# The first NSA scores ahead of the last query columns, and FoX output, compression and convolution in one block on TensorE

## The chip, the cores and the metric

The kernel runs on one core of a Trainium2 chip. The metric is the device time of one launch in microseconds (us), lower is better. A core has TensorE (PE, matrix products into PSUM), VectorE (DVE), ScalarE (ACT), GpSimd (POOL) and SyncE (SP, which here issues nearly all DMAs). Each engine works through its own list of instructions and waits on the others by semaphores.

## The reference

Two layers over 256 tokens of width 1024. Per layer:

```python
h = rms_norm(x, norm_g)
z = h @ w_in                                   # all inputs of three groups of heads
o_a = fox_attention(fq, fk, fv, ff + fox_b)    # 4 heads of 64, forget-gate bias, causal
o_b = conformer_conv(glu_in, ...)              # GLU, causal depthwise convolution of 31 taps
                                               # on 256 channels, LayerNorm, swish, 256x256 product
o_c = nsa_attention(...)                       # 8 query heads in 2 KV groups; three branches
                                               # mixed by sigmoid gates: compressed blocks,
                                               # selected blocks, sliding window
mixed = concatenate([o_a * silu(f_gate), o_b * silu(c_gate), o_c * silu(n_gate)])
x = x + mixed @ w_out
```

In the compressed branch, blocks of 32 keys (or values) at a stride of 16 go through a two-layer network with GELU, `gelu(blk @ w1) @ w2`; the 15 results are keys and values of their own. At 256 tokens the selected blocks and the window both cover all causal keys. A last RMSNorm follows. All is float32 at the interface.

## The kernel before

Large products are made in three terms of fp32r operands: weights and activations are split into a high and a low part (ACT casts the high part, L238; DVE subtracts for the low part, L242). The input projection is 24 column blocks of 128, each made by `s(i)` (L446 to L459): 24 matmuls of 128x256 into half a PSUM bank, two blocks to a bank. `s(16)` to `s(23)` are the blocks of the SiLU gates.

Weights come by one SP queue in a fixed list (`S_ORDER`, L169). They land in a ring of 6 raw buffers of 512 KB (`RAW`, L19). `pump()` (L214) issues the next load as soon as a raw buffer is free, which is when DVE has made the low part, or, for the weights `w1` of the compression, which are used unsplit, when `compress` has read them. The list has the eight `w1` pieces (four for the keys, four for the values) between blocks S11 and S16. So six of them are in the ring when the compression starts; the last two (`ww_1_2`, `ww_1_3`) and S16, S17, and so on, can only be issued while it runs.

Three steps are made of fp32 matmuls that fill only part of the columns of TensorE's array, several side by side:

- `fox_pv()` (L723): probabilities times values of FoX, 64 columns wide, 8 matmuls.
- `compress(i)` (L784): `w1` for keys (i=0) and values (i=1), 32 wide, 16 matmuls each, 4 to a `w1` piece. ACT then copies the result to `part` (L795).
- `conv()` (L539): the convolution, 32 wide, 64 matmuls.

The records count each fp32 matmul twice (x32, x16 and x128). `hidden()` (L803) multiplies `part` by a small matrix (the two halves of `part`, keys and values, have separate matmuls) and starts GELU on DVE and ACT, `gelu()` ends it, `compressed_kv()` (L823) applies `w2` (tile `pkv`), and `compressed()` (L835) makes the tiles `kcx` and `vbd` of the compressed keys and values, which `cmp_scores(0)` (tile `cs`, in pass n == 2) reads.

`scores(n)` makes the logits of query heads j = n mod 4 of both groups (tile `sw`), `exps(n)` the maximum on DVE and the exponentials on ACT, `norms(n)` the scaling on DVE, `trans(n)` the transposes on TensorE (tile `pt`), `pv(n)` the product with the values (tile `on`). Heads 0 and 1 need `query(0)`, which follows blocks S8 and S9; heads 2 and 3 need `query(1)`, after S10 and S11.

The order on PE, SP and POOL is that of the code. DVE and ACT are ordered by a scheduler that works from modelled times; `mark()` and `behind()` keep the splits from being put too early.

Of the kernel before, what the change touches and what calls it, by code (L numbers as in the profile page):

```python
# [124 lines left out]
def trunk(ctx, tc, a, out, dbg=None):  # L125
# [126 lines left out]
    def need(key, ahead=AHEAD):  # L252

        while key not in split:
            assert split_next(), key
        n = sum(1 for k in split)
        while n < ahead + 1 and split_next():
            n += 1
        return split[key]
# [139 lines left out]
    for l in range(L):  # L399
# [46 lines left out]
        def s(i, ahead=AHEAD):  # L446

            mark()
            hi, lo = need(("S", i, l), ahead)
            if i % 2 == 0:  # L450
                bank[i // 2] = pz(nm(f"ps{i}"))
            o = bank[i // 2][:, (i % 2) * 256:(i % 2 + 1) * 256]
            hi = hi.rearrange("p (k c) -> p k c", k=8)
            lo = lo.rearrange("p (k c) -> p k c", k=8)
            for k in range(8):
                te.matmul(o, hi[:, k], hTh[:, k], start=k == 0, stop=False)  # L456
                te.matmul(o, hi[:, k], hTl[:, k], start=False, stop=False)  # L457
                te.matmul(o, lo[:, k], hTh[:, k], start=False, stop=k == 7)  # L458
            del split["S", i, l]  # L459
# [263 lines left out]
        def fox_pv():  # L723
            ofv = fx["o"] = po(nm("ofx")).rearrange("p (i t) -> p i t", i=2)
            for i in range(2):
                for c, kt in ((slice(0, 256), 0), (slice(256, 384), 1)):
                    for g in range(2):
                        vc = slice((2 * i + g) * 64, (2 * i + g) * 64 + 64)
                        te.matmul(ofv[g * 64:(g + 1) * 64, i, kt * 128:], fv[:, kt, vc], fpts[i, g][:, c],
                                  start=i == 0 and kt == 0, stop=i == 1 and kt == 1)  # L730
# [20 lines left out]
        def query(i):  # L751

            if not qs2:
                qs2.extend(cp.tile([128, 4, 256], F32R, name=nm(f"qs{g}"), tag=f"qs{g}", bufs=1) for g in range(2))
            q = rope(s2(8 + 2 * i), C("ck").unsqueeze(1).broadcast_to([128, 2, 256]),
                     C("sk").unsqueeze(1).broadcast_to([128, 2, 256]), (2, 256), f"q{i}")
            for g, (r, r2) in enumerate(halves):
                hi = qs2[g][r, 2 * i:2 * i + 2]
                sc.mul(hi, q[r], 0.125)
                ve.scalar_tensor_tensor(qs2[g][r2, 2 * i:2 * i + 2], q[r], 0.125, hi.bitcast(F32), op0=ALU.mult,  # L760
                                        op1=ALU.subtract)
# [22 lines left out]
        def compress(i):  # L784

            ph = pscore(nm(f"ph{i}"))
            for q in range(4):
                w = raws.pop(("w1", i, q, l)).rearrange("p (k c) -> p k c", k=4)
                for j in range(4):
                    te.matmul(ph[j * 32:(j + 1) * 32, :256], cm["x", i][:, q * 4 + j, :], w[:, j, :],  # L790
                              start=q == 0, stop=q == 3)
                used(1)
            if i == 0:
                cm["part"] = cp.tile([128, 2, 256], F32, name=nm("part"), tag="tg", bufs=1)
            sc.copy(cm["part"][:, i], ph[:, :256])  # L795
# [7 lines left out]
        def hidden():  # L803
            hT = ppt(nm("hidT"))
            for i in range(2):
                for m in range(2):
                    te.matmul(hT[:, i * 64 + m * 32:i * 64 + m * 32 + 32], cm["part"][:, i, m * 128:(m + 1) * 128],
                              C("s4"), start=True, stop=True)
            ve.tensor_copy(hid, hT[:, :128])
            ve.tensor_tensor(g1, hid, hid, op=ALU.mult)  # L810
            ve.tensor_scalar(g1, g1, 0.044715, 1.0, op0=ALU.mult, op1=ALU.add)
            ve.tensor_tensor(g1, g1, hid, op=ALU.mult)
            sc.activation(g2, g1, AF.Tanh, scale=GELU_C)

        def gelu():
            ve.scalar_tensor_tensor(gk.rearrange("p m c -> p (m c)"), g2[:, 0:64], 1.0, hid[:, 0:64],
                                    op0=ALU.add, op1=ALU.mult)
            hv = hid[:, 64:128].rearrange("p (m n) -> p m n", n=16)
            tv = g2[:, 64:128].rearrange("p (m n) -> p m n", n=16)
            ve.scalar_tensor_tensor(tv, tv, 1.0, hv, op0=ALU.add, op1=ALU.mult)  # L820
            ve.tensor_copy(gv, tv.unsqueeze(2).broadcast_to([128, 4, 4, 16]))
# [51 lines left out]
        def exps(n, gs=(0, 1)):  # L873
            t = n // 4
            nk = 128 * (t + 1)
            if gs[0] == 0:
                Ps[n] = cp.tile([128, 2, 2, nk], F32, name=nm(f"P{n}"), tag="P", bufs=3)
                mxs[n] = cp.tile([128, 4], F32, name=nm(f"mx{n}"), tag="mx", bufs=4)
                sus[n] = cp.tile([128, 4], F32, name=nm(f"su{n}"), tag="su", bufs=4)
            P, mx, su = Ps[n], mxs[n], sus[n]  # L880
            msk = C("mk")[:, 0:128] if t == 0 else C("mk")[:, 128:384]
            for g in gs:
                for b in range(2):
                    c = 2 * g + b
                    masked(P[:, g, b], sb[n][g][b], msk, mx[:, c:c + 1])
                    sc.activation(P[:, g, b], P[:, g, b], AF.Exp, bias=mx[:, c:c + 1], scale=-1.0,  # L886
                                  accum_out=su[:, c:c + 1])
# [174 lines left out]
        keys_split()  # L1062
        s(1)
        blocks()
        s(10, 1)
        compress(0)
        fox_pv()
        compress(1)
        s(11, 1)
        query(1)  # L1070
        hidden()
        gelu()
        load_g(a["norm_g"][1] if l == 0 else a["final_g"], nm("gn"))
        scores(0)
        scores(1)
        exps(0)
        norms(0)
        exps(1)
        need(("S", 17, l), 0)
        conv()  # L1080
        cs = {}
        for n in range(8):
            t = n // 4
            trans(n)
            if n < 7:
                norms(n + 1)
            if n < 2:
                scores(n + 2)
            elif n < 6:
                scores(n + 2, (0,))  # L1090
            if n == 0:
                s(16)
                ln_stats()
                compressed_kv()
                compressed()
                exps(2)
                s(17)
                gates(0)
                mixed(0, 2, fx["o"], 0.5)
            elif n == 1:  # L1100
                s(18)
                exps(3)
                s(19)
                ln_swish()
                gates(1)
            elif n == 2:
                s(20)
                cs[0] = cmp_scores(0)
                exps(4, (0,))
                scores(4, (1,))  # L1110
                s(21)
                pcv = pointwise()
                gates(2)
                mixed(2, 2, pcv, 0.25)
                exps(4, (1,))
            elif n == 3:
                s(22)
                cmp_norm(0, *cs[0])
                exps(5, (0,))
                scores(5, (1,))  # L1120
                s(23)
                cmp_trans(0, cs[0][0])
                mix_split(0, 2)
                mix_split(2, 2)
                gates(3)
                exps(5, (1,))
                cs[1] = cmp_scores(1)
            else:
                if n % 2 == 0:
                    pj = pz(nm(f"pw0{n}"))  # L1130
                if n < 6:
                    need(("O", 2 * n - 3, l), 0)
                    exps(n + 2, (0,))
                ks = range(4) if n % 2 == 0 else range(4, 8)
                project(0, n // 2 - 2, pj, ks[:2])
                if n < 6:
                    scores(n + 2, (1,))
                    exps(n + 2, (1,))
                project(0, n // 2 - 2, pj, ks[2:])
            if n == 4:  # L1140
                cmp_norm(1, *cs[1])
            elif n == 6:
                cmp_trans(1, cs[1][0])
            if n % 2:
                pv(n - 1)
                pv(n)
            if n == 3:
                pv_cmp(0)
                mixed(4, 4, on[0], 0.5, slice(0, 128))
                mix_split(4, 4, slice(0, 128))  # L1150
            if n in (5, 7):
                residual(0, (n - 5) // 2 * 512, 512, pj)
# [96 lines left out]
```

## Time and profile before

| | |
|---|---|
| median of 3 runs | 317.46 us (317.41 to 318.85) |
| the profiled execution | 317.38 us, its span 315.6 us |
| mean granted TensorE clock | 0.997 |
| busy: PE, DVE, ACT, POOL | 304.8, 235.4, 187.1, 22.5 us |
| HBM read | 52.85 MB, 173 GB/s over the span |

The span runs from the first to the last instruction; 1.78 us lie around it. A matmul's busy time is that of one instruction with its fill, and successive matmuls overlap; what a step costs on TensorE is read from the start of its first matmul to the start of the next step's first. The two layers have the same order; times below are of the first.

### The profile page before, as it was taken

Reading aid. Unit: us, or ns where it says so; the run is one execution under the profiler, and the core shown is the slowest. Engines: PE = TensorE matmul, PEld = TensorE weight load, DVE = VectorE, ACT = ScalarE, POOL = GpSimd, SP = SyncE. Lnnn points to the kernel's source line nnn. Section 1 sums busy time; section 2 is a strip of 40 time slices with the busy share of each in tenths; the row PEclk is TensorE's granted clock in tenths of the full one; section 3 lists DMA queues with packets and bytes.
Section 4 is the critical chain, followed back from the end, with each engine's and each line's share of the span. In section 5 each row is a group of like instructions: output and inputs, shape, how many; then the busy total and the mean of one; then the engine's idle time right before and its main releaser. Section 6 shows DMA issues by size and latency. Waiting matters only on the chain.

```text
span 315.6 us, 6707 instructions
## 1 busy us (share of the span) xinstructions
PE 304.8 (97%) x2590; PEld 273.3 (87%) x2590; DVE 235.4 (75%) x627; ACT 187.1 (59%) x408; POOL 22.5 (7%) x50
## 2 busy tenths in 40 slices
PE   8899999999999999999999999999999999999991
PEld 3799999995879999888899999999577999988891
DVE  3847789982799998974573778998199999896532
ACT  4647669650495958761554766874159595786110
POOL 2000034000002000000000003400000200000000
PEclk9999999999999999999999999999999999999998
DMA  7697798905937444230452778880791744000101
GB/s 289 220 382 262 262 256 212 353 3 214 413 111 265 136 135 132 68 93 2 153 180 102 255 251 272 211 316 2 260 409 71 264 133 135 0 2 0 56 15 68
DMA packets 16547, 54.93 MB, mean 174 GB/s; under 512 B 2049, under 2 KB 2433, under 8 KB 16514
## 3 DMA queue, kind: packets, MB, share of 16 engines
q1 hardware_dynamic: 15408, 51.51, 46.6%
q0 software_dynamic: 960, 2.92, 4.1%
q8 instruction: 20, 0.33, 0.4%
q14 instruction: 13, 0.11, 0.1%
q10 hardware_dynamic: 146, 0.07, 0.1%
HBM read 52.85 MB, written 1.64 MB: 173 GB/s over the span
## 4 chain that ended last, share of the span: by engine, by line
PE 89%; issue 4%; DMA 3%; ACT 1%; DVE 1%; POOLq 0%; POOL 0%; DVEq 0%
PE ps L456 15%; PE ps L458 14%; PE ps L457 14%; PE pcn L545 4%; PE pA L429 4%; PE pt L914 4%; PE pB L429 4%; PE pw L977 4%; PE pw L978 4%; PE pw L981 4%; PE on L927 3%; DMA ww<-in_w 3%; PE sw L858 2%; PE sw L859 2%; PE fpt L718 1%
## 5 line engine op out<-in xcount | busy, mean ns | idle before, releaser
L456 PE MATMUL ps<-hTh,wS_1h 128*128 128x256 f32 x192 | 54.4, 283 | 0.0
L456 PE MATMUL ps<-hTh,wS_0h 128*128 128x256 f32 x192 | 54.3, 283 | 0.0
L458 PE MATMUL ps<-hTh,wS_0l 128*128 128x256 f32 x192 | 54.0, 281 | 0.0
L458 PE MATMUL ps<-hTh,wS_1l 128*128 128x256 f32 x192 | 54.0, 281 | 0.0
L457 PE MATMUL ps<-hTl,wS_1h 128*128 128x256 f32 x192 | 54.0, 281 | 0.0
L457 PE MATMUL ps<-hTl,wS_0h 128*128 128x256 f32 x192 | 54.0, 281 | 0.0
L886 ACT ACTIVATE P<-P,mx 128x128 f32<-128x128 f32 (+1 forms) x64 | 28.5, 448 | 15.1 <-DVE mx L481 15.0
L456 PEld LDWEIGHTS ps<-hTh,wS_1h 128*128 128x128 f32 x192 | 36.2, 189 | 0.6 <-issue 0.4
L456 PEld LDWEIGHTS ps<-hTh,wS_0h 128*128 128x128 f32 x192 | 36.2, 189 | 0.6 <-issue 0.4
L457 PEld LDWEIGHTS ps<-hTl,wS_0h 128*128 128x128 f32 x192 | 36.2, 189 | 0.2
L457 PEld LDWEIGHTS ps<-hTl,wS_1h 128*128 128x128 f32 x192 | 36.2, 189 | 0.2
L458 PEld LDWEIGHTS ps<-hTh,wS_1l 128*128 128x128 f32 x192 | 36.2, 189 | 0.0
L458 PEld LDWEIGHTS ps<-hTh,wS_0l 128*128 128x128 f32 x192 | 36.2, 189 | 0.0
L242 DVE TENSOR_TENSOR wS_0l<-wS,wS_0h 128x1024 fp32r<-128x1024 f32 x24 | 28.5, 1220 | 8.3 <-ACT wS_0h L238 8.3
L242 DVE TENSOR_TENSOR wS_1l<-wS,wS_1h 128x1024 fp32r<-128x1024 f32 x24 | 28.5, 1221 | 8.0 <-ACT wS_1h L238 8.0
L238 ACT CAST wS_1h<-wS 128x1024 fp32r<-128x1024 f32 x24 | 24.1, 1052 | 1.8 <-DMA wS<-in_wS 1.8
L238 ACT CAST wS_0h<-wS 128x1024 fp32r<-128x1024 f32 x24 | 24.1, 1051 | 0.5 <-DMA wS<-in_wS 0.4
L481 DVE CUSTOM_DVE_ANT_0 P<-sw,cf 128x128 f32<-128x128 f32 (+1 forms) x64 | 19.4, 354 | 2.4 <-PE sw L859 2.4
L916 ACT COPY PT<-pt 128x512 f32<-128x512 f32 x24 | 13.6, 585 | 9.6 <-PE pt L914 9.6
L984 DVE TENSOR_TENSOR x<-pw,x 128x512 f32<-128x512 f32 (+1 forms) x9 | 5.7, 630 | 16.7 <-PE pw L981 16.7
L484 DVE TENSOR_SCALAR P<-P,co 128x128 f32<-128x128 f32 (+1 forms) x64 | 16.4, 316 | 0.1
L545 PE MATMUL pcn<-yr,cw 128*32 128x256 f32 x256 | 14.2, 380 | 0.0
(241 smaller groups left out, 680.5 us busy)
## 6 DMA issues: line engine op xcount, KB each, us to landing
wS<-in_wS SPq DMA_DIRECT2D x48, 512.0 KB, 5.7
ww<-in_w SPq DMA_DIRECT2D x16, 512.0 KB, 4.8
wO<-in_wo SPq DMA_DIRECT2D x16, 512.0 KB, 3.6
yr<-ybuf POOLq DMA_DIRECT2D x16, 142.0 KB, 5.7
wA<-in_wA SPq DMA_DIRECT2D x4, 420.0 KB, 5.2
wB<-in_wB SPq DMA_DIRECT2D x4, 390.0 KB, 3.9
x<-in_x SPq DMA_DIRECT2D x2, 512.0 KB, 4.1
w<-in_w SPq DMA_DIRECT2D x2, 384.0 KB, 4.4
```

The lines of the kernel that those rows point to most:

```text
L238: behind(E.Activation, lambda: sc.copy(hi, w))
L242: behind(E.DVE, lambda: ve.tensor_tensor(lo, w, hi.bitcast(F32), op=ALU.subtract))
L429: te.matmul(p[:, :n], a_[:, k, tok], b_, start=first, stop=s_ == "t" and k == 7)
L456: te.matmul(o, hi[:, k], hTh[:, k], start=k == 0, stop=False)
L457: te.matmul(o, hi[:, k], hTl[:, k], start=False, stop=False)
L458: te.matmul(o, lo[:, k], hTh[:, k], start=False, stop=k == 7)
L481: ve.tensor_tensor_reduce(o, x, m, -1.0, 3.0e38, ALU.add, ALU.min, mx)
L484: ve.tensor_scalar(x, x, r, None, op0=ALU.mult)
L545: te.matmul(p[g * 32:(g + 1) * 32, i * 256:(i + 1) * 256], w[:, g, q], yr[:, g, 4 * q:4 * q + 256], start=q == 0, stop=q == 7)
L886: sc.activation(P[:, g, b], P[:, g, b], AF.Exp, bias=mx[:, c:c + 1], scale=-1.0, accum_out=su[:, c:c + 1])
L914: te.transpose(pt[:, o + b * 128:o + (b + 1) * 128], Pg[:, b * 128:(b + 1) * 128], C("id"))
L916: sc.copy(PT, pt)
```

## The change

Only the order of calls in the layer's loop changes. The first two score steps with their exponentials move from behind `gelu()` to ahead of `s(10)`; `fox_pv`, both `compress` and `conv` follow `s(11)` in a row, with `conv` between the two `compress`; `hidden` follows them directly; and `compressed_kv`, `compressed` move from pass n == 0 to pass n == 1, between `s(18)` and `s(19)`.

```diff
         blocks()
-        s(10, 1)
-        compress(0)
-        fox_pv()
-        compress(1)
-        s(11, 1)
-        query(1)
-        hidden()
-        gelu()
         load_g(a["norm_g"][1] if l == 0 else a["final_g"], nm("gn"))
         scores(0)
         scores(1)
         exps(0)
         norms(0)
         exps(1)
+        s(10, 1)
+        s(11, 1)
+        query(1)
+        fox_pv()
+        compress(0)
+        conv()
+        compress(1)
+        hidden()
+        gelu()
         need(("S", 17, l), 0)
-        conv()
...
             if n == 0:
                 s(16)
                 ln_stats()
-                compressed_kv()
-                compressed()
                 exps(2)
...
             elif n == 1:
                 s(18)
+                compressed_kv()
+                compressed()
                 exps(3)
                 s(19)
```

On PE of the first layer, around the narrow steps, stood before (`ph` is the result of a compression, `ww` a piece of `w1`, `ofx` the FoX output, `ps` a projection block):

```order
L458 MATMUL ps_0_966<-hTh,wS_0l 128x256
L790 MATMUL ph_0_991<-ww_0_0_0_590,xp_0_954 32x256 x4
...
L729 MATMUL ofx_1018<-fPT_0_858,fv_125 64x256
...
L790 MATMUL ph_0_1027<-ww_1_0_0_687,xp_0_960 32x256 x4
...
L790 MATMUL ph_0_1027<-ww_1_2_0_996,xp_0_960 32x256 x4
L790 MATMUL ph_0_1027<-ww_1_3_0_1002,xp_0_960 32x256 x4
L456 MATMUL ps_0_966<-hTh,wS_0h 128x256
```

And now, at the same place (`sw` are the scores, `pcn` the convolution, `hidT` the product of `hidden`, `pt` the transposes of pass n == 0):

```order
L859 MATMUL sw_0_973<-klz_115,qs_0_872 128x256
L456 MATMUL ps_0_1008<-hTh,wS_0h 128x256
...
L729 MATMUL ofx_1067<-fPT_0_858,fv_125 64x256
...
L790 MATMUL ph_0_1076<-ww_0_0_0_590,xp_0_954 32x256 x4
...
L545 MATMUL pcn_1103<-yr_0_427,cw_584 32x256 x32
L545 MATMUL pcn_1103<-yr_0_505,cw_584 32x256 x32
L790 MATMUL ph_0_1171<-ww_1_0_0_687,xp_0_960 32x256 x4
...
L790 MATMUL ph_0_1171<-ww_1_3_0_1087,xp_0_960 32x256 x4
L807 MATMUL hidT_1197<-cf,part_1101 128x32 x4
L914 MATMUL pt_0_1222<-cf,P_0_978 128x128 x4
```

The whole convolution now lies between the first compression, which frees the raw buffers, and the second, which needs the two pieces loaded into them; and the matmuls of `hidden` follow the second compression at once.

On ACT of the first layer, at the same place, stood before:

```order
L759 ACTIVATE qs_0_872<-q0u_874 64x512
L795 COPY part_1016<-ph_0_991 128x256
L795 COPY part_1016<-ph_0_1027 128x256
L238 CAST wS_0h<-wS_0_1008 128x1024
L238 CAST wS_0h<-wS_0_1014 128x1024
L886 ACTIVATE P_0_1118,su_0_1120<-P_0_1118,mx_0_1119 128x128 x4
```

And now (`wS_0_1093` and `wS_0_1099` are the raw blocks S16 and S17, `wS_0_1176` is S18, `yc` the convolution's result, `P_0_1302` the probabilities of head 2):

```order
L886 ACTIVATE P_0_997,su_0_999<-P_0_997,mx_0_998 128x128 x4
L795 COPY part_1101<-ph_0_1076 128x256
L759 ACTIVATE qs_0_871<-q1u_1058 64x512
L759 ACTIVATE qs_0_872<-q1u_1058 64x512
L238 CAST wS_0h<-wS_0_1093 128x1024
L238 CAST wS_0h<-wS_0_1099 128x1024
L549 ACTIVATE yc_128<-pcn_1103,sm_92 128x256 x2
L795 COPY part_1101<-ph_0_1171 128x256
L916 COPY PT_0_1223<-pt_0_1222 128x512
L238 CAST wS_0h<-wS_0_1176 128x1024
...
L886 ACTIVATE P_0_1302,su_0_1304<-P_0_1302,mx_0_1303 128x128 x2
```

The casts of S16 and S17, which wait for their DMAs, stand ahead of the eviction of the convolution and of the second copy to `part`; those of S18 to S20 stand ahead of the exponentials of head 2. POOL's list is the same; on SP the load of the next norm's factors (`gn`) moves from behind the seventh block after the compression to ahead of `ww_1_2`.

## Rows read from the trace of the kernel before

**Rows 1.** The page: busy time, share of the span and instructions of each engine.

```profile
PE 304.8 (97%) x2590; PEld 273.3 (87%) x2590; DVE 235.4 (75%) x627; ACT 187.1 (59%) x408; POOL 22.5 (7%) x50
```

**Rows 2.** Waits of PE: waiter, releaser, us in total, times, longest.

```profile
PE ph L790 <- DMA ww<-in_w: 1.3, 2, 0.7
```

**Rows 3.** The chain that ended last, first compression: start, us, what.

```profile
73.66 4.36 DMA ww<-in_w
```

**Rows 4.** Timeline of PE, 72.3 to 78.9: start, us, line, tiles, forms, count, idle before.

```profile
72.32 0.28 PE L458 MATMUL ps<-hTh,wS_0l 128*128 128x256 f32 x1
72.53 1.93 PE L790 MATMUL ph<-ww,xp 128*32 128x256 f32 x32
74.39 1.52 PE L729 MATMUL ofx<-fPT,fv 128*64 128x256 f32 x16
75.84 1.58 PE L790 MATMUL ph<-ww,xp 128*32 128x256 f32 x24
78.07 0.64 PE L790 MATMUL ph<-ww,xp 128*32 128x256 f32 x8 [0.65 <-DMA ww<-in_w]
78.64 0.39 PE L456 MATMUL ps<-hTh,wS_0h 128*128 128x256 f32 x1
```

**Rows 5.** Timeline of PE, hidden to pass n == 0.

```profile
81.58 0.97 PE L807 MATMUL hidT<-cf,part 128*128 128x32 f32 x8
82.39 0.36 PE L858 MATMUL sw<-kh,qs 128*128 128x256 f32 x1
...
83.50 7.11 PE L545 MATMUL pcn<-yr,cw 128*32 128x256 f32 x128
90.55 0.66 PE L914 MATMUL pt<-cf,P 128*128 128x128 f32 x4
90.96 0.36 PE L858 MATMUL sw<-kh,qs 128*128 128x256 f32 x1
...
91.63 0.28 PE L456 MATMUL ps<-hTh,wS_0h 128*128 128x256 f32 x1
```

**Rows 6.** Timeline of PE, passes n == 0 to n == 2.

```profile
94.47 0.60 PE L562 MATMUL lnp<-cf,yc 128*128 128x128 f32 x4
95.00 0.42 PE L829 MATMUL pkv<-gk,w 128*64 128x16 f32 x8
...
95.81 0.37 PE L456 MATMUL ps<-hTh,wS_0h 128*128 128x256 f32 x1
...
98.73 0.60 PE L914 MATMUL pt<-cf,P 128*128 128x128 f32 x4
99.09 0.36 PE L858 MATMUL sw<-kh,qs 128*128 128x256 f32 x1
...
99.64 0.28 PE L456 MATMUL ps<-hTh,wS_0h 128*128 128x256 f32 x1
...
110.67 0.96 PE L938 MATMUL cs<-kcx,qs 128*128 128x32 f32 x8
```

**Rows 7.** Timeline of ACT, 78 to 108.

```profile
78.77 0.37 ACT L795 COPY part<-ph 128x256 f32<-128x256 f32 x1 [3.87 <-PE ph L790]
79.32 1.05 ACT L238 CAST wS_0h<-wS 128x1024 fp32r<-128x1024 f32 x1 [0.18 <-DMA wS<-in_wS]
80.60 1.05 ACT L238 CAST wS_0h<-wS 128x1024 fp32r<-128x1024 f32 x1 [0.23 <-DMA wS<-in_wS]
...
107.55 0.43 ACT L841 CAST kcx<-kcx 64x16 fp32r<-64x16 f32 x2
```

**Rows 8.** Timeline of DVE, 68 to 81.

```profile
68.13 1.39 DVE L760 SCALAR_TENSOR_TENSOR qs<-q0u,qs 64x512 fp32r<-64x512 f32 x2 [1.10 <-ACT qs L759]
...
80.40 1.22 DVE L242 TENSOR_TENSOR wS_0l<-wS,wS_0h 128x1024 fp32r<-128x1024 f32 x1 [7.17 <-ACT wS_0h L238]
```

**Rows 9.** Timeline of SP's queue: start, us, line, transfer, count.

```profile
73.23 0.80 SPq L223 DMA_DIRECT2D ww<-in_w  x2
```

**Rows 10.** Windows: stretch, us, busy (instructions) of each engine, clock, DMA share, GB/s.

```profile
65.00:70.00 5.00, 5.00 (x43) 4.74 (x42) 3.53 (x9) 2.31 (x5) 0.00 (x0) 1.00 0.01 3
```

## The prediction

> **What bounds the kernel now.** I read the engine totals first: PE is busy 97% of the span, DVE 75%, ACT 59% [rows 1]. So time can only come from PE's few gaps, and from places where it is busy but not at its pace. The waits of PE have one entry in this stretch: the compression waits for its weights, 1.3 us in total in 2 waits, one to a layer [rows 2]. The chain shows the same DMA with 4.36 us [rows 3], but that is its whole way from the release of its buffer to the landing. While it flies PE does the rest of the compression and the FoX output; only what is left is lost. The timeline of PE tells how much, by starts of steps [rows 4, 5].
>
> **Pace.** One projection block is 2.84 us where nothing disturbs it (91.63 to 94.47, 24 matmuls [rows 5, 6]), 118 ns a matmul. The same narrow form has two undisturbed lengths: the first compression, 32 records in 1.86 us (72.53 to 74.39), and the convolution, 128 records in 7.05 us (83.50 to 90.55) [rows 4, 5]. The difference is 5.19 us for 96 records, 54.1 ns each, and leaves 1.86 - 32 x 0.0541 = 0.13 us fixed for each narrow step.
>
> **The change, part by part (per layer).**
>
> 1. The weight wait. The second compression takes 2.80 us (75.84 to 78.64) where the first takes 1.86 [rows 4]. 0.94 us is lost, more than the 0.65 that stands as idle. Now 128 records of convolution, 6.93 us, lie between the first compression and the second. The two late pieces landed by 78.07, which is 5.54 us after the first compression began [rows 4]; from the new beginning to the second compression there are 1.73 + 6.93 = 8.66 us. They are 3.1 us early. Gain 0.94.
> 2. One block of narrow steps. First compression, convolution and second compression have one width and follow each other: 192 x 0.0541 + 0.13 = 10.52 us, against 1.86 + 1.86 + 7.05 = 10.77. Gain 0.25. If each step keeps its fixed part, it is 0.
> 3. Changes between narrow and full width. S11 after the second compression takes 2.94 us (78.64 to 81.58), 0.10 over its pace [rows 4, 5]. The eight score matmuls take 1.11 us (82.39 to 83.50), between `hidden` and the convolution; at 117 ns each they would be 0.93 [rows 5]. Among projection blocks both lose this: gain 0.28. The step from full width into the first narrow one, 0.09 (72.32 to 72.53 instead of 0.12 later [rows 4]), stays.
> 4. `hidden` now follows the second compression at once, and its second half needs ACT's copy. Before, S11 covered it, 2.94 us. The copy starts 0.13 us after the next step began and takes 0.37 [rows 4, 7], so 0.5 us, and a semaphore more. The first four matmuls of `hidden`, half of 0.81 us [rows 5], use the first copy and can run meanwhile. Cost between 0.1 and, if the first half hides nothing and the weights, which are `part` itself, must be loaded after the copy, about 0.75. I take 0.2, since the two halves wait separately. What is behind `hidden` on PE, the transposes and scores of pass n == 0, waits with it; its other inputs are ready.
> 5. Scores ahead of S10. They start when S(1) ends, at 72.53 - 2.93 = 69.60. Their queries are ready when DVE has written the second half, at 68.13 + 1.39 = 69.52 [rows 8], and the matmuls of that half are two matmuls in, at 69.83. Cost 0, with 0.3 us to spare. DVE stands idle for 7.17 us ahead of 80.40 [rows 8], so maxima, scaling and the second query rope find a free engine, where before they crowded beside the convolution. The scores of pass n == 0 took 0.67 us (90.96 to 91.63) against 0.55 one pass later (99.09 to 99.64) [rows 5, 6]: they had waited for the second query, which is now early. Gain 0.12. The norm factors' load moves to where the DMA engines are idle, share 0.01 [rows 10]: 0.
> 6. `compressed_kv` between S18 and S19: the 0.81 us (95.00 to 95.81) stays. Before, it shared its return to full width with the transposes `lnp` ahead of it, and S17 took 2.92 (95.81 to 98.73) [rows 6], which those transposes will still cause. Now it has its own way in and out, 0.08 to 0.17. I take 0.12.
> 7. The compressed keys. From the end of `pkv` to `cs` PE had 14.86 us (95.81 to 110.67) [rows 6]; now S19 and what follows it up to the end of S20 lie between: from the start of S18 it was 11.03 (99.64 to 110.67), less 2.84 for S18 itself, 8.2. `kcx` was ready at 107.55 + 0.43, 12.2 us after `pkv` [rows 6, 7], but most of that was queueing behind work that nobody hurried. If none of the queueing came back the wait would be 0, if all, 4.0 us. In the new order the last step stands on ACT and DVE behind the LayerNorm's activations, one transposed copy and one weight split, which end about when S20 does. I take 0.2.
>
> Sum per layer: 0.94 + 0.25 + 0.28 + 0.12 - 0.2 - 0.12 - 0.2 = 1.07 us; two layers 2.14. From the profiled execution, 317.38, that gives 315.2 us; it is 0.08 under the median of the runs shown, so nothing is added.
>
> The weights that come later are the cover that could go. The narrow block begins with the FoX output at 69.60 + 0.93 + 2 x 2.84 + 0.09 = 76.30, the first compression at 77.75, 5.22 later than before. S16 and S17 were there at 79.32 and 80.60 [rows 7], the fourth transfer 7.4 us after the first issue at 73.23 [rows 9], 1.28 us apart. Shifted they come at 84.5 and 85.8; their casts end at 86.9, under the second compression (86.4 to 88.3), so the copy to `part` isn't held. S18 can be issued only 0.7 us into that compression, at 87.1, and by the same steps lands at about 90.7, S20 at 93.2. The exponentials of head 2 stand behind these casts on ACT and start some 0.7 us later against PE than before. They are needed two passes on.
>
> On that: ACT shows such a cast idle until its DMA with other work queued behind [rows 7]. The Trainium skill, "TensorE: Matmul & The Clock Gate", the table of specifications, says that the ScalarE and VectorE queues are strictly first in, first out, while TensorE may pull weight loads ahead. By that rule a late S16 would hold back the convolution's eviction and `part`, and a late S20 the exponentials; by the landings above the first costs nothing and the second is inside the slack, so the sum stays, and the rule sharpens the rival below.
>
> **Rivals.**
>
> - *Smaller gain, new waits.* `hidden` costs 0.75 and `cs` 0.7: 0.94 + 0.25 + 0.28 - 0.75 - 0.17 - 0.7 + 0.12 = -0.03 a layer, or about 0.5 if only one comes. Time 316.3 to 317.4. For it: `hidden` has no cover at all now, and DVE is the second busiest engine [rows 1]. Against: the halves of `part` are waited for apart.
> - *The block gains nothing by being one.* If each narrow step keeps its fixed 0.13 us, and full-width steps theirs, because every PSUM tile starts with its own semaphores: part 2 and half of part 3 go; 0.68 a layer is left, 316.0 us. Against: the fixed part has the same size as the steps at a change of width.
> - *Slower: the compressed keys arrive late.* `kcx` is queued on ACT and DVE behind work that waits for late weights and for `lnq`. Each us that it is later than the end of S20 costs PE one, twice. With the full 4.0 us of part 7 instead of 0.2 the kernel is at 317.38 + 2 x (4.0 - 1.27) = 322.8; it gets slower by 0.5% once the wait passes 2.1 us a layer. For it: 12.2 us then, 8.2 now. Against: the queue on DVE is shorter, since 7 us of work moved into idle time.
>
> **How the numbers follow.** Forecast 0.56 (314.6 to 315.7), no block gain 0.16, smaller gain 0.20, late keys 0.08. 0.5%, 1.6 us, is about what a measurement of this kernel tells from no change, so faster means under 315.9: the forecast and a half of the second, 0.64; same 0.29; slower 0.07. With parts 4, 6 and 7 at their low ends a layer gains 1.41 and the time is 314.6; the range begins at 314.4, since the part of the pace that comes from two lengths can be off by 0.1 a layer. Upward the range takes in the second rival and most of the smaller gain, to 316.8.
>
> **What would show it.** Right: no wait of PE for `ww`; the second compression at 1.86 us; convolution and both compressions within 10.6 us from start to start; `hidden` 0.1 to 0.3 us behind its place; `cs` within 0.4 us of the end of S20; transposes of pass n == 0 about 1.3 us earlier than 90.55. Wrong: a wait of `hidden` above 0.5, of `lnq` for DVE, of `cs` for `kcx` above 0.7, or of any projection block for a cast.

## The result: 321.46 us, slower

Six runs of the changed kernel gave a median of 321.46 us (319.96 to 322.93), six of the kernel before on the same chip 317.55 (317.36 to 318.85). The ratio is 1.010, with a 95% interval of 1.007 to 1.013. The forecast was 315.2 with a range to 316.8, and slower had 0.07. The forecast was wrong in sign.

The profiled execution took 321.47 us; its span is 319.7, 4.1 more than before. I read the totals first, then the waits of PE. The totals of the page, which answer to [rows 1]:

```profile
PE 306.2 (96%) x2590; PEld 276.0 (86%) x2590; DVE 236.9 (74%) x627; ACT 187.7 (59%) x408; POOL 20.7 (6%) x50
```

The waits of PE after (waiter, releaser, us in total, times, longest):

```profile
PE lnq L578 <- DVE yn L570: 2.3, 2, 1.2
PE cs L938 <- DVE kcx L840: 1.9, 2, 0.9
...
PE hidT L807 <- ACT part L795: 0.3, 1, 0.3
```

The wait for `ww` of [rows 2] is gone, as forecast. Two others stand in its place, each once a layer: `lnq`, the transposes of the normalised convolution result, waits for `yn`, and `cs` for the compressed keys `kcx`.

The timeline of PE shows that the half of the stage with the narrow steps did what it should (start, us, line, tiles, forms, count; answers to [rows 4, 5]):

```profile
77.49 1.52 PE L729 MATMUL ofx<-fPT,fv 128*64 128x256 f32 x16
78.94 1.93 PE L790 MATMUL ph<-ww,xp 128*32 128x256 f32 x32
80.69 7.09 PE L545 MATMUL pcn<-yr,cw 128*32 128x256 f32 x128
87.60 1.91 PE L790 MATMUL ph<-ww,xp 128*32 128x256 f32 x32
89.44 1.19 PE L807 MATMUL hidT<-cf,part 128*128 128x32 f32 x8
90.47 0.63 PE L914 MATMUL pt<-cf,P 128*128 128x128 f32 x4
```

From start to start, the second compression is 1.84 us (2.80 before), the three steps of one width 10.50 (78.94 to 89.44; forecast 10.52), `hidden` 1.03. S(1) ended at 70.77, so from there to the transposes of pass n == 0 it is 19.70 us; before it was 20.95 (69.60 to 90.55). That is -1.25 us, where parts 1 to 4 of the forecast sum to -1.27 in a layer.

The next rows of the same timeline show the loss (in brackets: idle before, and what ended it; they answer to [rows 6]):

```profile
101.36 0.42 PE L829 MATMUL pkv<-gk,w 128*64 128x16 f32 x8
...
102.17 0.37 PE L456 MATMUL ps<-hTh,wS_0h 128*128 128x256 f32 x1
...
106.51 0.80 PE L578 MATMUL lnq<-cf,yn 128*128 128x128 f32 x4 [1.24 <-DVE yn L570]
...
109.22 0.28 PE L456 MATMUL ps<-hTh,wS_0h 128*128 128x256 f32 x1
...
113.15 1.04 PE L938 MATMUL cs<-kcx,qs 128*128 128x32 f32 x8 [0.94 <-DVE kcx L840]
```

S19, now the block behind `pkv`, lasts from 102.17 to 106.51, 4.34 us; before, the block behind `pkv` was S17 and took 2.92. S20 lasts from 109.22 to 113.15, 3.93 us instead of 2.84. The way from the transposes to `cs` is 22.68 us, 20.12 before. So the first layer loses 2.56 and gains 1.25, together +1.3. The second layer, counted in the same way, comes out at +1.5; there `hidden` waits 0.30 us for the copy to `part`. Another 1.2 us was lost near the start, ahead of the first changed instruction, where eight transposes and the products around them ran slowly in this execution (the last section). Two of the six executions of the kernel before lie about that much above the rest too (318.51 and 318.85 beside 317.36 to 317.65), so I do not put it to the change. 1.3 + 1.5 + 1.2 is 4.0 of the 4.1. So the trace gives the change 2.8 us and not the whole 3.9 between the medians; why two executions of the changed kernel took 322.76 and 322.93 no trace shows.

Why is `yn` late? The timeline of ACT after, the casts of S16 to S20 and what follows them (answers to [rows 7]):

```profile
86.44 1.04 ACT L238 CAST wS_0h<-wS 128x1024 fp32r<-128x1024 f32 x1 [3.60 <-DMA wS<-in_wS]
87.64 1.05 ACT L238 CAST wS_0h<-wS 128x1024 fp32r<-128x1024 f32 x1 [0.16 <-DMA wS<-in_wS]
...
92.18 1.05 ACT L238 CAST wS_0h<-wS 128x1024 fp32r<-128x1024 f32 x1 [0.40 <-DMA wS<-in_wS]
94.46 1.05 ACT L238 CAST wS_0h<-wS 128x1024 fp32r<-128x1024 f32 x1 [1.23 <-DMA wS<-in_wS]
96.73 1.05 ACT L238 CAST wS_0h<-wS 128x1024 fp32r<-128x1024 f32 x1 [1.22 <-DMA wS<-in_wS]
97.69 0.40 ACT L886 ACTIVATE P<-P,mx 128x128 f32<-128x128 f32 x1
```

And of DVE after, from the first of these splits to `kcx`:

```profile
93.26 1.23 DVE L242 TENSOR_TENSOR wS_0l<-wS,wS_0h 128x1024 fp32r<-128x1024 f32 x1 [0.52 <-ACT wS_0h L238]
95.54 1.23 DVE L242 TENSOR_TENSOR wS_0l<-wS,wS_0h 128x1024 fp32r<-128x1024 f32 x1 [1.06 <-ACT wS_0h L238]
97.81 1.22 DVE L242 TENSOR_TENSOR wS_0l<-wS,wS_0h 128x1024 fp32r<-128x1024 f32 x1 [1.04 <-ACT wS_0h L238]
98.95 0.76 DVE L564 BATCH_NORM_STATS2 st<-lnp 128x6 f32<-128x256 f32 x2
...
105.82 1.00 DVE L570 TENSOR_SCALAR yn<-lnp,mv,rv 128x256 f32<-128x256 f32 x2
...
112.83 0.37 DVE L840 TENSOR_TENSOR kcx<-kcu,kcx 64x16 fp32r<-64x16 f32 x2
```

ACT waits for S18, S19 and S20, which come 2.27 us apart, and DVE waits with it, 2.6 us over the three splits. The LayerNorm's statistics, which had their input from `lnp` at 94.25 + 0.60, stand behind the third split and start at 98.95. From there DVE is busy without a break to `yn` and `kcx`. In the kernel before the three casts ran back to back; its rows of ACT, of DVE and of PE:

```profile
91.88 2.96 ACT L238 CAST wS_0h<-wS 128x1024 fp32r<-128x1024 f32 x3
94.72 0.41 ACT L886 ACTIVATE P<-P,mx 128x128 f32<-128x128 f32 x1
...
99.26 1.00 DVE L570 TENSOR_SCALAR yn<-lnp,mv,rv 128x256 f32<-128x256 f32 x2 [0.48 <-POOL rv L567]
...
105.32 0.60 PE L578 MATMUL lnq<-cf,yn 128*128 128x128 f32 x4
```

Where the loads themselves were held up is seen below.

### The profile page after: what moved, and what is told of

It is laid out like the page before. It is cut to its first block, busy times and chain, and to the rows that moved or that the text cites. A ratio compares the mean times of both kernels' runs of the same rounds, so it can differ in the third digit from the quotient of the medians.

```text
span 319.7 us, 6713 instructions
## 1 busy us (share of the span) xinstructions
PE 306.2 (96%) x2590; PEld 276.0 (86%) x2590; DVE 236.9 (74%) x627; ACT 187.7 (59%) x408; POOL 20.7 (6%) x50
## 3 DMA queue, kind: packets, MB, share of 16 engines
q0 software_dynamic: 960, 2.92, 3.9%
## 4 chain that ended last, share of the span: by engine, by line
PE 75%; DVE 8%; DMA 6%; issue 5%; ACT 4%; POOLq 0%; POOL 0%; SPq 0%; DVEq 0%
PE ps L456 11%; PE ps L457 11%; PE ps L458 11%; DMA wS<-in_wS 6%; PE pA L429 4%; PE pB L429 4%; PE pw L978 3%; PE pw L977 3%; PE pw L981 3%; PE pt L914 3%; PE on L927 2%; PE pcn L545 2%; PE ph L790 2%; PE hp L356 1%; PE sw L858 1%
## 5 line engine op out<-in xcount | busy, mean ns | idle before, releaser
L481 DVE CUSTOM_DVE_ANT_0 P<-sw,cf 128x128 f32<-128x128 f32 (+1 forms) x64 | 20.1, 354 | 3.5 <-PE sw L859 3.0
```

Source lines behind the costliest of these rows:

```text
L481: ve.tensor_tensor_reduce(o, x, m, -1.0, 3.0e38, ALU.add, ALU.min, mx)
```

## The experiments

Theory W (late weights): the first compression is moved back, so buffers come free late, S18 to S20 land late, and ACT's and DVE's queues pass that on to `yn` and `kcx`. Rival O (order): the loads are harmless; the new order that the scheduler gave ACT and DVE, and the later `compressed_kv`, put `yn` and `kcx` too far back. The lines below are of the first layer.

**The compressed keys back in pass n == 0** (the changed kernel otherwise).

```diff
             if n == 0:
                 s(16)
                 ln_stats()
+                compressed_kv()
+                compressed()
                 exps(2)
...
             elif n == 1:
                 s(18)
-                compressed_kv()
-                compressed()
```

> The changed kernel with compressed_kv and compressed put back into pass n == 0, behind the transposes lnp; all else as changed. Late-weights theory (S18 to S20 land after the second compression, their casts hold all that stands behind them on ACT and DVE): GELU's tanh stands behind those casts too, so gk is ready only some 5 us after PE reaches pkv; PE waits about 5 us a layer at pkv, the waits at lnq and cs go, and the kernel is slower than the changed one, 324 to 328 us. Order theory (the waits come from where the scheduler put yn and kcx on DVE and ACT, whatever the weights do): kcx and yn now stand earlier in DVE's list, the waits at lnq and cs go and nothing takes their place, 314.5 to 316 us.

330.22 us (328.31 to 330.51), ratio to before 1.036 (1.031 to 1.041). A timeline of PE:

```profile
94.69 0.60 PE L562 MATMUL lnp<-cf,yc 128*128 128x128 f32 x4
99.41 0.62 PE L829 MATMUL pkv<-gk,w 128*64 128x16 f32 x8 [4.11 <-DVE gk L816]
```

The last step of GELU (`gk`) sits behind the same late splits on DVE, and here PE has nothing else to do meanwhile. So the change's own move of `compressed_kv` was a cover, not a cost, and O is wrong on that point. PE now waits 8.0 us for `gk` where the changed kernel waited 4.5 in all, but 8.8 us more are lost, and the time is above the expected 324 to 328. At least part of the rest goes with the clock (the last section): in the profiled execution S17 takes 4.52 us (100.84 to 105.36) instead of 2.92, at a granted clock of 0.50 to 0.62.

**S16 and S17 ahead of the last two pieces of `w1` in the load list** (the changed kernel otherwise; ACT and DVE keep their order).

```diff
-    S_ORDER = (..., 10, 11, "w1", 16, 17, 18, ...)
+    S_ORDER = (..., 10, 11, "w1", 18, ...)
...
+                        if (m, q) == (1, 2):
+                            for j in (16, 17):
+                                queue.append((("S", j, l), a["wS"][l, j], 1024))
+                                parts.append((("S", j, l), 1024))
```

> The changed kernel with one edit to the list of loads: blocks S16 and S17 ahead of the last two pieces of w1. ACT's and DVE's lists keep the changed kernel's order. Late-weights theory: S16 and S17 land some 2.5 us earlier, their splits free two raw buffers before the second compression, S18 to S20 land by about 89 to 92 instead of 92 to 97 (us of the first layer), the exponentials of head 2 start about 3 us earlier, the waits at lnq (1.2) and cs (0.9) go, no wait for ww: 314.6 to 315.8 us. Order theory: the lists are unchanged, so the waits stay, 319.5 to 322 us.

316.42 us (314.73 to 317.76), ratio 0.993 (0.990 to 0.996). The only new waits of PE, and ACT's casts of S16 to S20 (lines are four further down in this kernel):

```profile
PE cs L942 <- DVE kcx L844: 1.3, 2, 0.9
```

```profile
83.27 1.05 ACT L242 CAST wS_0h<-wS 128x1024 fp32r<-128x1024 f32 x1 [1.63 <-DMA wS<-in_wS]
84.53 1.05 ACT L242 CAST wS_0h<-wS 128x1024 fp32r<-128x1024 f32 x1 [0.22 <-DMA wS<-in_wS]
90.46 2.03 ACT L242 CAST wS_0h<-wS 128x1024 fp32r<-128x1024 f32 x2
93.87 1.05 ACT L242 CAST wS_0h<-wS 128x1024 fp32r<-128x1024 f32 x1 [1.38 <-DMA wS<-in_wS]
```

S18 and S19 are there when ACT comes to them; only S20 is still late. `lnq` waits no more and `cs` waits less in total. That wait was expected to go altogether, and the time is 0.6 us above the expected range. With the same order of calls, a change in the list alone brings 5 us.

**The first compression ahead of S11, and the second ahead of the convolution** (the changed kernel otherwise). Below it is called the version with the first compression ahead of S11.

```diff
         s(10, 1)
+        compress(0)
         s(11, 1)
         query(1)
         fox_pv()
-        compress(0)
-        conv()
         compress(1)
+        conv()
         hidden()
```

> The changed kernel with compress(0) between S10 and S11 and compress(1) ahead of the convolution (order: scores, S10, compress(0), S11, fox_pv, compress(1), conv, hidden). The later part of ACT's and DVE's lists keeps the order. Late-weights theory: the raw buffers come free 5 to 9 us earlier, S18 to S20 land under the convolution, waits at lnq and cs go, the copy to part is covered by the convolution, one more pair of width changes costs 0.3 a layer: 314.8 to 316.2 us. Order theory: 319.5 to 322 us.

315.15 us (315.12 to 316.66), ratio 0.990 (0.986 to 0.994), span 313.4. None of the waits is left. ACT's casts of S18 to S20, `yn` and `kcx` on DVE, `cs` on PE:

```profile
90.67 2.94 ACT L238 CAST wS_0h<-wS 128x1024 fp32r<-128x1024 f32 x3
```

```profile
101.80 0.99 DVE L570 TENSOR_SCALAR yn<-lnp,mv,rv 128x256 f32<-128x256 f32 x2
...
109.16 0.36 DVE L840 TENSOR_TENSOR kcx<-kcu,kcx 64x16 fp32r<-64x16 f32 x2
```

```profile
104.13 0.60 PE L578 MATMUL lnq<-cf,yn 128*128 128x128 f32 x4
109.47 1.02 PE L938 MATMUL cs<-kcx,qs 128*128 128x32 f32 x8
```

From the copy of `hidT` to `yn` DVE has the same list in this kernel and in the changed one, instruction for instruction. Only the weights come in time: the three casts run back to back. From the transposes of pass n == 0, `yn` starts after 12.34 us (89.46 to 101.80), in the changed kernel after 15.35 (90.47 to 105.82). These 3.0 us are what the weights cost. But in the kernel before it was 8.71 (90.55 to 99.26), so the new order by itself takes 3.6 us of slack. O is half right: the order used up the slack, and the weights then went past it.

**Only the first scores moved** (the kernel before otherwise).

```diff
+        scores(0)
+        scores(1)
+        exps(0)
+        norms(0)
+        exps(1)
         s(10, 1)
         compress(0)
         fox_pv()
```

> The kernel before with one part of the change alone: the first two score steps ahead of S10. Both theories: the wait for ww stays at 0.65 a layer, the scores lose their two changes of width (0.18 a layer) and the second score step of pass n == 0 its wait (0.12): 316.6 to 317.4 us, no new waits. If it is slower than before, moving the scores is itself a cost that I have not seen.

318.47 us (317.09 to 319.02) beside 318.82 (317.50 to 320.77) of before, ratio 0.999 (0.996 to 1.001): no difference that can be measured. The wait for `ww` stays (1.4 us in total). The scores are neither the loss nor a gain by themselves.

**Both compressions ahead of the convolution** (the changed kernel otherwise).

```diff
         fox_pv()
         compress(0)
-        conv()
         compress(1)
+        conv()
         hidden()
```

> The changed kernel with the second compression ahead of the convolution again: FoX output, compression of the keys, compression of the values, convolution, hidden. Late weights: the last two pieces of w1 are needed 1.9 us after the first compression begins and are there some 5.5 us after it, so the second compression waits for them, 2 to 2.7 us a layer; the six buffers are read out when it ends, under seven us of convolution, so S18 to S20 land before pass n == 0 and the waits of the LayerNorm's transposes for yn and of cs for the compressed keys are gone. Gain 2 x 2.2, cost 2 x 2.5 of the changed kernel: 320 to 322.5 us, with one kind of wait in place of the other. Order alone (the scheduler's new places on ACT and DVE delay yn and the keys): these waits stay, with the new one on top, 325 to 327.

322.58 us (321.23 to 323.24), ratio 1.013 (1.009 to 1.017). Of the new waits of PE one is left, and the casts of S18 to S20 run without a gap again:

```profile
PE ph L790 <- DMA ww<-in_w: 5.5, 4, 2.8
```

```profile
95.89 2.95 ACT L238 CAST wS_0h<-wS 128x1024 fp32r<-128x1024 f32 x3
```

As W has it: one wait for weights replaces the others. (Not all of the time is waiting: the convolution ran slowly behind the wait, as the last section shows.) Where the convolution covers the two pieces of `w1`, nothing covers S18 to S20; where it covers S18 to S20, nothing covers the pieces.

**The first compression ahead of the FoX output**, 1.45 us earlier (the changed kernel otherwise).

```diff
-        fox_pv()
         compress(0)
+        fox_pv()
         conv()
         compress(1)
```

> The changed kernel with the compression of the keys ahead of the FoX output in the same block, 1.45 us earlier; nothing else moves. Late weights: the buffers come free 1.45 us sooner, but S18 and S19 still take the buffers of S16 and S17; S18 to S20 land 0.7 to 1.45 us sooner and the waits at lnp and cs, 1.2 and 0.9 us a layer at their longest, shrink by about that: 318 to 320 (between the changed kernel, 321.5, and the one with the first compression a whole block earlier, 315.2). Order alone: nothing changes, 321 to 322.

318.52 us (316.64 to 320.60), ratio 1.001 (0.998 to 1.004): between the changed kernel and the one with the compression a whole step earlier. The waits of PE:

```profile
PE cs L938 <- DVE kcx L840: 0.9, 1, 0.9
PE lnq L578 <- ACT tg L493: 0.7, 1, 0.7
```

Each now stands once, in the second layer, where S20's cast starts 5.75 us after the transposes (237.48 to 243.23) and `yn` 14.84 us (237.48 to 252.32), between the 12.34 and the 15.35 above. (The view puts this wait of `lnq` down to `tg` on ACT, which ended at 253.00; in the version with the compression ahead of S11 `lnq` starts before `tg` does, 104.13 and 104.38, so `yn` is the likelier releaser.) In the first layer it starts 3.43 us after them (89.40 to 92.83) and nothing waits. In the changed kernel it was 6.26 (90.47 to 96.73), in the version with the compression ahead of S11 about 3.2, with no wait. The kernel with the other list of loads lies between: 4.62 (89.25 to 93.87), no wait at `lnq`, 0.87 us at `cs`. A dose with its response, and within one kernel a layer with and one without.

**The good version, with the compressed keys back in pass n == 0.** The same diff as in the first experiment, on the version with the compression ahead of S11.

> The version with the first compression ahead of S11, but with compressed_kv back in pass n == 0, ahead of S17. Late weights: nothing is late here, but gelu's last step on DVE (gk) ended at 95.8 to 96.1 us in that version's trace, behind three weight splits in a row, and pkv would be reached at about 93.6 (after the transposes lnp), so pkv waits about 2.3 us a layer; then 315.2 + 4.6 = 319 to 320, and up to 1 us more if PE runs slowly after the wait, as it did in the changed kernel with the same step back. If instead DVE's order follows the code and gk comes ahead of the splits: no wait, 315 to 315.6, and the move of compressed_kv was not needed.

323.28 us (323.09 to 326.93), ratio 1.015 (1.011 to 1.019). PE's waits, and the stretches around the first (us, busy and count of PE, PEld, DVE, ACT and POOL, granted clock, DMA share, GB/s):

```profile
PE pkv L829 <- DVE gk L816: 4.5, 2, 2.2
```

```profile
94.50:97.30 2.80, 0.58 (x6) 0.35 (x4) 2.80 (x6) 2.80 (x11) 0.00 (x0) 0.95 0.71 202
97.30:98.80 1.50, 1.47 (x13) 1.44 (x13) 1.50 (x6) 0.23 (x1) 0.00 (x0) 0.50 0.97 300
98.80:101.00 2.20, 2.20 (x11) 2.20 (x12) 2.12 (x12) 0.00 (x0) 0.73 (x1) 0.50 0.92 309
101.00:104.00 3.00, 3.00 (x17) 3.00 (x16) 1.38 (x8) 0.81 (x4) 0.00 (x0) 0.52 0.35 139
104.00:107.00 3.00, 3.00 (x27) 3.00 (x26) 2.22 (x11) 2.82 (x8) 0.00 (x0) 1.00 0.00 0
```

The wait is 2.25 us, as expected (2.3). The time is 3 us above the expectation: the rows show the granted clock at 0.50, the lower of its two levels (1.2 GHz, where 1.00 is 2.4), from 97.3 to close to 104, and S17 takes 5.19 us (98.76 to 103.95). The profiled execution is the slowest of the five, 326.93 us; the others took 323.09 to 323.35, so these rows show more than the median lost. Moving `compressed_kv` behind S18 is thus needed even where no weight is late, since the splits of S18 to S20 stand ahead of `gk` on DVE.

## Why the prediction was wrong

- Parts 1, 2, 3 and 5 hold. No wait for `ww`; 10.50 us for the three steps of one width (10.52 forecast); the stretch from S(1) to the transposes 1.25 shorter; and from the transposes to S16 0.94 us (90.47 to 91.41) instead of 1.08. The version with the compression ahead of S11 has no late weights, and its span is 2.2 us under that of before, 1.1 a layer.
- Part 4 holds in the first layer: `hidden` takes 1.03 instead of 0.81 (0.2 forecast). In the second it takes 1.39, with a wait of 0.30 for the copy to `part`; that is inside the 0.75 allowed for it, but not the 0.2 taken.
- Part 6 holds roughly: in the good version S18 takes 2.94 us and S19 2.93 around `pkv`, 0.19 over their pace of 2.84 each; 0.12 was forecast.
- Part 7 is right where the weights are in time: in the good version `kcx`, written by two instructions, ends at 109.52, and `cs` starts at 109.47, where S20 ends. There is no slack left in it. In the changed kernel `cs` waits 0.94 us where the sum has 0.2.
- **The step that failed is the paragraph on the cover**: "S18 can be issued only 0.7 us into that compression, at 87.1, and by the same steps lands at about 90.7, S20 at 93.2. The exponentials of head 2 stand behind these casts on ACT and start some 0.7 us later against PE than before. They are needed two passes on." Two things in it are off. First the size: the exponentials started 7.22 us after the transposes (90.47 to 97.69) instead of 4.17, so 3.05 later and not 0.7 (before: 90.55 to 94.72). With the 1.2 us of the start taken off, S18 was cast at 91.0, nearly as forecast, but S20 at 95.6 instead of 93.2. Second the slack: what is behind the casts is not only the exponentials of head 2. It is also DVE's queue with the LayerNorm's statistics and `yn`, needed one pass on. The sum has no term for that wait, which is 1.24 us in the first layer. In the kernel before `yn` started at 99.26 for an `lnq` at 105.32, 6.06 us ahead; the new order had already used 3.6 us of that, and where no weight is late 2.33 are left (101.80 to 104.13).
- Why the landing was late. I took S18's buffer to be freed by the second compression. But SP, between 85 and 95, waited for DVE's splits:

```profile
SPq L223 <- DVE wS_0l L242: 5.0, 3, 2.3
```

  DVE split S16 and S17 from 87.51 to 89.95, and S18 and S19 were issued at 88.77 and 89.98, as the one and the other ended. So the chain is: late first compression, late pieces, late S16 and S17, and their splits give the buffers for S18 and S19. Against the forecast, though, this chain costs little: with the 1.2 us taken off, S18 was issued at 87.6 instead of 87.1. S18 was there 3.4 us after its issue, S19 4.5 and S20 6.3 after theirs, so they came 2.27 us apart where I had used 1.28; that is 2.0 of the 2.4 us by which S20 is late. The rates (us, busy of the engines, clock, DMA share, GB/s of the changed kernel):

```profile
90.00:93.00 3.00, 3.00 (x27) 3.00 (x27) 1.95 (x12) 1.41 (x2) 0.00 (x0) 1.00 0.77 249
93.00:96.00 3.00, 3.00 (x28) 3.00 (x28) 1.68 (x2) 1.28 (x2) 0.00 (x0) 1.00 0.98 397
96.00:100.00 4.00, 4.00 (x37) 4.00 (x36) 2.96 (x8) 3.27 (x11) 0.00 (x0) 1.00 1.03 414
```

  At 414 GB/s a block of 512 KB is 1.27 us, near that 1.28. In the first stretch it is 249. In the second it is 397, and still S20 came 2.27 us after S19: the first two rows add up to 1.9 MB, 3.7 blocks, and by 96 only S18 and S19 had landed. So loads issued behind S20 (up to 92.22) were being moved beside it. Why the rate is low at first, and why the loads did not land one after the other at 1.28 us as S16 and S17 had before, is open; no run tells it apart.
- The rival that came true is the third, the compressed keys late "behind work that waits for late weights and for `lnq`", priced to decide from 2.1 us a layer. The two waits, with what they cost around them, are 2.56 us. It got 0.08 because I let that work end "about when S20 does", and did not follow the lateness of S20's weights through DVE's list.
- The rule quoted in the prediction from the Trainium skill ("TensorE: Matmul & The Clock Gate", the table of specifications: ACT and DVE take their work strictly in order) agrees with the runs: in the changed kernel the statistics, with their input there by 94.85, wait behind the split at 97.81. The forecast had weighed by it the exponentials alone, and not what stands behind the splits on DVE.

## What to carry to other kernels

When a step that frees buffers is moved back, follow every load behind it, buffer by buffer, to who frees that buffer now, and then follow the lateness through the in-order queues of the engines that unpack the load, down to what PE waits for. Take the slack from the new order, not from the old one. Here the loads wanted the first compression early and the second late; splitting the two around S11 and the FoX output gave 315.15 us, 0.990 of the kernel before, where the same calls in one block gave 321.46, 1.010 of it.

## What had not been expected of the hardware

- After one wait of PE of 2.25 us the granted clock was 0.50 from 97.3 to close to 104, and after one of 4.11 us as well (99.4 to 102.5); in the second layers of these two executions it was 0.50 again, from 251 to 257 and from 255 to 258. With both compressions ahead of the convolution, waits of 2.80 and 0.64 us were followed by windows of 0.63 (85 to 87) and 0.52 (87 to 89), and the convolution took 8.71 us instead of 6.91. In the second layer of the same execution the waits were 1.39 and 0.63 us, and the clock stayed at 1.00. After the waits of 1.24 and 0.94 us of the changed kernel it stayed at 1.00. So here two waits of about 1 us cost 2.56 us a layer, and one of 2.25 us some 4.1 by the medians ((323.28 - 315.15) / 2), more in the profiled execution.
- The slow stretch near the start stands in the profiled executions of four kernels (the changed one, both with the compressed keys in pass n == 0, and the one with only the scores moved) and not in the other five, before among them. The windows show the granted clock at 1.00 there, but 51 or 52 records instead of 62 in nine us (the changed kernel, then the kernel before):

```profile
11.00:20.00 9.00, 8.44 (x52) 8.21 (x53) 8.07 (x13) 4.72 (x9) 0.00 (x0) 1.00 0.71 250
```

```profile
11.00:20.00 9.00, 8.30 (x62) 7.81 (x63) 8.01 (x14) 5.14 (x11) 0.00 (x0) 1.00 0.69 240
```

  Its cause is open. It limits what one execution can tell to somewhat over 1 us, which is why the single steps were compared from S(1) on.
